# Seven-product down groups of a four-layer trunk: where the weight sums and the negated token factors stand in VectorE's order, when their loads are queued, and where ScalarE copies a first product in blocks five to eight

## The chip, the cores and the metric

One core of a Trainium2 chip runs the whole program. The time is device microseconds from one execution of the program; a run's number is a median over executions, and the kernel before was run three times. The engines that appear below are TensorE (PE; its weight loads are PEld), VectorE (DVE), ScalarE (ACT), GpSimd (POOL) and SyncE (SP). Each takes its own instructions in order. SP issues the plain loads; POOL issues the loads that add what they bring to what lies in the buffer.

## The reference

A trunk of four layers on 512 tokens of width 1024, in fp32. Each layer is a mixer (S5, gated linear attention, differential attention, S5) and then a SwiGLU feed-forward part; only the latter is touched here:

```python
def swiglu_ffn(h, w_gate_up, w_down):
    g, u = jnp.split(h @ w_gate_up, 2, axis=-1)
    return (jax.nn.silu(g) * u) @ w_down
...
        h = rmsnorm(x, norm_ffn[layer])
        x = x + swiglu_ffn(h, ffn_w_gate_up[layer], ffn_w_down[layer]).astype(x.dtype)
```

The hidden width is 2816, w_gate_up is 1024 x 5632, w_down 2816 x 1024.

## The kernel before

**Precision.** A product of fp32 matrices is made of three matmuls on rounded values: each operand is split into a high part (a rounding copy on ScalarE, L420 for weights) and a low part (the rest, a subtraction on VectorE, L428), and high x high, high x low and low x high are summed in PSUM. So each tile of weights of 128 x 1024 needs one ScalarE copy and one VectorE subtraction (`split`) before TensorE can use it.

**Blocks.** `ffn` handles the 2816 hidden columns in 11 blocks of 256. The gate and up columns of a block are computed together by `seven_block`: the two halves of the tokens and the two halves of the depth make a 2 x 2 block product, which is done with seven products and not eight (`seven_product`, L594), by sums of weights and of activations. The products are named by the method's steps: `one` writes bank a, `two` bank d, `five` bank c, and so on; the functions ending in `_out` take a bank away. In `one_out` ScalarE copies bank a to r1 (L816), `two_out` adds bank d to r1 on VectorE (L823), and `scale1` multiplies r1 by the token factors (L786).

**Down groups.** The blocks are gathered in groups of 4, 4 and 3, and each group is multiplied with its rows of w_down and added to x. In layers 2 and 3 the first two groups (blocks 0 to 3 and 4 to 7) use seven products here too (`seven_down`, L1113 for the matmuls); there `raw(b)` is the room of the block's results. Its weights are named by the same method: `1` is a sum of two quarters, made by a plain load and an accumulating load by POOL; `S` first takes a quarter and then, on VectorE, the tile `1` is added to it (L1131, "the weight sums", two tiles of 128 x 1024 per group). `11`, `21`, `22`, `3` are the others. `parts` splits the activations (L1102 on ScalarE, L1104 on VectorE). `add` adds a bank to x with the token factors r, or with their negative nr (L1154); in layer 2 r is first turned through memory (the tile rturned, brought back by a transfer), in layer 3 it stands in memory already.

**What sets the order.** The program is written in the order of the steps; a scheduler then places each instruction on its engine by what it depends on, and `issue_after` ties an instruction behind another. In the third and later blocks of `ffn` the steps come in the order of the loops that the printed code shows; `early`, `sums`, `before` and `products` are the four pieces of a down group. Loads go to SP in the order of the program's steps. A load can start when its buffer is free. The buffers are `wst` (a ring of three staged tiles), `whl` (a ring of five split tiles), and a list `slots` of eight tiles that are taken and handed back (slot0, slot1, slot2, gain, and four that are pieces of the tile halves). Matmul results go to PSUM: four banks of one kind (a, c, a2, c2), two of another (d, d2).

Of the kernel before, what the change touches and what calls it, by code (L numbers as in the profile page):

```python
# [12 lines left out]
F32 = mybir.dt.float32  # L13
# [9 lines left out]
P = 128  # L23
# [317 lines left out]
class Trunk:  # L341
# [387 lines left out]
    def seven_block(self, fp, slots, left, wgu, b, turn, na, glued, raw=None):  # L729
# [83 lines left out]

        def one_out():
            keep["r1"] = third("r1")
            nc.scalar.copy(keep["r1"][:], bank["a"][:])  # L816

        def two():
            bank["d"] = self.sbank("d")
            product("12", "21", bank["d"], True)  # L820

        def two_out():
            v.tensor_tensor(keep["r1"][:], keep["r1"][:], bank["d"][:], op=ALU.add)  # L823

        def scale1():
            scale(keep["r1"], keep["r1"], 0)
# [75 lines left out]
    def ffn(self, l, left, after=None, turn=False, aside=None, small=None):  # L902
# [7 lines left out]
        with self.tc.tile_pool(name=f"ffn{l}", bufs=1, reuse_waits="tile") as fp:  # L910
# [88 lines left out]
            for nb in (4, 4, 3) if na == 4 else (3, 3, 3, 2):  # L999
                acts = []  # L1000
                down = self.seven_down(fp, slots, rooms, wd, b0, r, na, turn) if b0 < halved else None
                for n in range(b0, b0 + nb):
                    b = blocks[n]
                    if down and n == max(b0 + 2, 3):
                        down["early"]()
# [11 lines left out]
                    if n > 2 or l == 1 and n == 2:  # L1017
                        loads(b)
                        for step in ("one", "one_out", "five", "five_out"):
                            b[step]()  # L1020
                        b["add"]("22")
                    if n > 1:
                        for step in ("six", "six_out", "two", "two_out", "scale1", "silu1", "seven", "seven_out", "three", "three_out"):
                            b[step]()
                        b["add"]("21")
                        if down and n == b0 + 3:
                            down["sums"]()
                        b["four"]()
                        if down and n == b0 + 3:
                            down["before"]()  # L1030
                        for step in ("gate2", "times"):
                            b[step]()
# [27 lines left out]
    def seven_down(self, fp, slots, rooms, wd, b0, r, na, turn):  # L1060
# [66 lines left out]
        def early():  # L1127
            load("1", 0, 1, (0, 0), True)
            load("S", 1, 1, None, True)
            for w, y in zip(W["1"], W["S"]):  # L1130
                v.tensor_tensor(y, w, y, op=ALU.add)  # L1131
# [6 lines left out]
        def sums():  # L1138
            load("11", 0, 0)
            load("21", 1, 0, None, True)  # L1140
# [7 lines left out]
        def products():  # L1148
# [4 lines left out]
            nr = self.sp.tile([P, NT], F32, tag="ms4", name="nr", bufs=2)  # L1153
            v.tensor_scalar_mul(nr[:], r[:], -1.0)  # L1154
# [6 lines left out]
            freed("21")  # L1161
# [3 lines left out]
            add(0, 0, a, r)  # L1165
            d = [self.sbank("d2") for _ in range(2)]
# [30 lines left out]
        return {"early": early, "before": before, "sums": sums, "products": products}  # L1197
# [1924 lines left out]
```

## Time and profile before

| what | value |
|---|---|
| median of 3 runs | 2228.75 us (2226.74 to 2230.62) |
| profiled execution, its own time | 2231.23 us |
| its span | 2229.5 us |
| mean granted TensorE clock | 0.992 of full speed |
| bytes moved by transfers | 354.67 MB, mean 159 GB/s |
| first down group, layer 2, from the end of blocks 0 and 1 | 1400 to 1515 us |
| second down group, layer 2 | 1515 to 1634.7 us |
| first down group, layer 3 (its end) | 1912 to 2008.8 us |
| second down group, layer 3 | 2008.8 to 2131.6 us |

A row of the timeline has the start, the length, engine, line, operation, written and read tile; brackets hold the idle time ahead of it and what ended it. A row of the waits has a total, the times and the longest. The windows give per stretch the length, the busy time of TensorE, its weight loads, VectorE, ScalarE and GpSimd with their counts, the granted clock, the busy share of the transfer engines, and GB/s. A row of the transfers has the number, the size and the median us from issue to landing.

### The profile page before, as it was taken

How to read it: one execution, taken by the hardware profiler on the slowest of the kernel's cores; microseconds unless marked ns; L12 is line 12 of the kernel's file. 1: busy time of each engine (PE TensorE's matmuls, PEld its weight loads, DVE VectorE, ACT ScalarE, POOL GpSimd, SP SyncE). 2: the span in 40 equal slices, each digit the busy share in tenths (PEclk: the TensorE clock that was granted, in tenths of full speed). 3: DMA queues.
4: the chain of work that ended last, by engine and by line, in shares of the span. 5: the costliest groups of instructions: out<-in, count | busy, mean ns of one | idle time of the engine just before them, and what ended most of it. 6: DMA issues, size and time to landing. Idle time of an engine off the chain costs nothing.

```text
span 2229.5 us, 38518 instructions
## 1 busy us (share of the span) xinstructions
PE 2156.1 (97%) x15313; PEld 1958.4 (88%) x15313; DVE 1707.8 (77%) x2588; ACT 1173.6 (53%) x1852; POOL 360.9 (16%) x467
## 2 busy tenths in 40 slices
PE   6999999999999999999999999899999999999998
PEld 5888989989988898999888888799998888889997
DVE  9965978777987597877645786797986965897885
ACT  8644635445666465564435785454553334554553
POOL 3401152340210110100002221111110001111100
PEclk9999999999999999999999999899999999999999
DMA  4357667665863686764347556979762646788752
GB/s 92 64 173 179 175 160 189 171 172 161 189 142 124 151 205 165 172 186 117 96 135 163 119 130 170 233 205 215 199 168 58 161 142 159 190 224 186 203 146 76
DMA packets 320101, 354.67 MB, mean 159 GB/s; under 512 B 71220, under 2 KB 253648, under 8 KB 319794
## 3 DMA queue, kind: packets, MB, share of 16 engines
q1 hardware_dynamic: 243362, 247.39, 36.7%
q0 software_dynamic: 76560, 104.82, 25.3%
q8 instruction: 121, 1.98, 0.4%
q14 instruction: 58, 0.48, 0.1%
HBM read 318.20 MB, written 18.75 MB: 151 GB/s over the span
## 4 chain that ended last, share of the span: by engine, by line
PE 77%; DVE 10%; DMA 5%; ACT 4%; issue 3%; SPq 1%; POOL 0%; DVEq 0%; POOLq 0%; ACTq 0%
PE a L594 20%; PE c L594 9%; PE acc L448 8%; PE acc L450 8%; PE acc L449 8%; PE d L594 5%; DVE whl L428 3%; PE a L1113 2%; PE y L1860 2%; PE acc L1896 2%; PE c L1113 1%; ACT whl L420 1%; DMA gain<-in_ffn_w_down_dram 1%; PE s L2868 1%; DMA halves<-in_ffn_w_down_dram 1%
## 5 line engine op out<-in xcount | busy, mean ns | idle before, releaser
L428 DVE TENSOR_TENSOR whl<-wst,whl 128x1024 fp32r<-128x1024 f32 x244 | 296.8, 1222 | 181.3 <-ACT whl L420 178.3
L594 PE MATMUL a<-side,whl 128*128 128x256 f32 x3240 | 401.6, 281 | 22.0 <-DVE whl L428 15.3
L594 PEld LDWEIGHTS a<-side,whl 128*128 128x128 f32 x3240 | 387.8, 192 | 25.1 <-DVE whl L428 17.1
L420 ACT CAST whl<-wst 128x1024 fp32r<-128x1024 f32 x244 | 255.5, 1051 | 203.1 <-PE acc L450 115.4
L594 PE MATMUL c<-side,whl 128*128 128x256 f32 x2160 | 263.2, 279 | 7.1 <-DVE g L786 5.5
L594 PEld LDWEIGHTS c<-side,whl 128*128 128x128 f32 x2160 | 255.2, 189 | 7.6 <-issue 5.6
L428 DVE TENSOR_TENSOR whl<-slot,whl 128x1024 fp32r<-128x1024 f32 x121 | 146.9, 1221 | 39.7 <-ACT whl L420 39.6
L448 PE MATMUL acc<-whl,act 128*128 128x512 f32 x448 | 176.1, 394 | 0.4 <-ACT whl L420 0.4
L449 PE MATMUL acc<-whl,act 128*128 128x512 f32 x448 | 174.9, 390 | 0.0
L450 PE MATMUL acc<-whl,act 128*128 128x512 f32 x448 | 174.8, 390 | 0.0
L420 ACT CAST whl<-slot 128x1024 fp32r<-128x1024 f32 x121 | 126.7, 1052 | 86.2 <-DVE slot L840 28.4
L420 ACT CAST whl<-halves 128x1024 fp32r<-128x1024 f32 x103 | 107.5, 1051 | 90.4 <-DVE halves L840 38.8
L428 DVE TENSOR_TENSOR whl<-halves,whl 128x1024 fp32r<-128x1024 f32 x103 | 125.0, 1221 | 25.2 <-ACT whl L420 24.5
L594 PE MATMUL a<-sides,whl 128*128 128x256 f32 x1080 | 132.8, 279 | 0.6 <-DVE x L576 0.6
L594 PE MATMUL d<-sides,whl 128*128 128x256 f32 x1080 | 132.0, 278 | 0.4 <-ACT whl L420 0.4
L594 PEld LDWEIGHTS a<-sides,whl 128*128 128x128 f32 x1080 | 128.6, 189 | 1.7 <-issue 1.0
L594 PEld LDWEIGHTS d<-sides,whl 128*128 128x128 f32 x1080 | 128.1, 188 | 0.6 <-ACT whl L420 0.6
L448 PEld LDWEIGHTS acc<-whl,act 128*128 128x128 f32 x448 | 84.0, 188 | 19.0 <-ACT whl L420 0.6
L450 PEld LDWEIGHTS acc<-whl,act 128*128 128x128 f32 x448 | 84.1, 188 | 17.7
L775 POOL DMA_DIRECT2D wst<-in_ffn_w_gate_up_dram x44 | 56.9, 1293 | 258.1 <-DMA wst<-in_ffn_w_gate_up_dram 94.0
L449 PEld LDWEIGHTS acc<-whl,act 128*128 128x128 f32 x448 | 84.2, 188 | 16.5
L1113 PE MATMUL a<-whl,part 128*128 128x512 f32 x384 | 89.7, 389 | 0.0
(565 smaller groups left out, 4399.2 us busy)
## 6 DMA issues: line engine op xcount, KB each, us to landing
wst<-in_ffn_w_gate_up_dram SPq DMA_DIRECT2D x88, 512.0 KB, 5.3
slot<-in_ffn_w_gate_up_dram SPq DMA_DIRECT2D x75, 512.0 KB, 5.4
wst<-in_ffn_w_down_dram SPq DMA_DIRECT2D x72, 512.0 KB, 4.6
wst<-in_ffn_w_gate_up_dram POOLq DMA_DIRECT2D x44, 512.0 KB, 6.9
halves<-in_ffn_w_gate_up_dram SPq DMA_DIRECT2D x36, 512.0 KB, 5.8
wst<-in_s_w_glu_dram SPq DMA_DIRECT2D x32, 512.0 KB, 4.8
wst<-in_diff_w_qkv_dram SPq DMA_DIRECT2D x24, 512.0 KB, 3.8
slot<-in_ffn_w_gate_up_dram POOLq DMA_DIRECT2D x16, 512.0 KB, 8.1
```

What stands on the lines that cost most here:

```text
L420: self.last["high"] = self.nc.scalar.copy(hl[:, 0], w[:])
L428: self.last["low"] = self.nc.vector.tensor_tensor(hl[:, 1], w[:], hl[:, 0].bitcast(F32), op=ALU.subtract)
L448: mm(out, lh, rh, start=first, stop=False)
L449: mm(out, lh, rl, start=False, stop=False)
L450: self.last["mm"] = mm(out, ll, rh, start=False, stop=last)
L594: mm(o, *two, start=first and not (j or k or n), stop=k == 3 and n == 2, skip_group_check=True,)
L775: nc.gpsimd.dma_start(w[:], left.quarter(*plus, b), accum_op=ALU.add)
L1113: self.last["mm"] = nc.tensor.matmul(banks[t][:], o[:, y, k, ts], hl[:, z, k % 2], start=first and not (k or n), stop=k == 3 and n == 2, s ...
L1860: mm(yb[:, b], q[:, j, b], om[:, j // 2, bs(b)], start=False, stop=j == 3)
L1896: mm(accs[t][:], zT[:, m // 2, kk, t * P : (t + 1) * P], hl[:, m % 2, kk % 2], start=kk == 0 and m == 0, stop=kk == KT - 1 and m == 2,)
L2868: nc.tensor.matmul(ss[m][:], qs[:, m, ts], ks[:, m, z], start=z == 0, stop=z == 1)
```

## The change

- `early` (the part 11 and the differences s3) is called at the third block of each group; for the first group this is one block earlier. The loads of `1` and `S` leave it; a new function `weights` holds them and is called at the group's last block, after that block's gate-up loads.
- The sums S = 1 + S leave `early` too and are made in `sums`, which is now called after `four` and not before it, and are tied behind the last weight subtraction issued by then (`last["low"]`).
- The weights `21` come through the staging ring and no longer through slots, so `freed("21")` is gone.
- nr is made after the parts 2 and tied behind their last subtraction.
- In blocks 4 to 7 (counted from 0) of layers 2 and 3 ScalarE copies bank a into bank d, the product of `two` is accumulated on it, `two_out` has no instruction, and `scale1` reads bank d.

```diff
--- before.py
+++ after.py
@@ -811,19 +811,29 @@
             bank["a"] = self.acc("a")
             product("11", "11", bank["a"], True)
 
+        upon = raw is not None and b > 3
+
         def one_out():
-            keep["r1"] = third("r1")
-            nc.scalar.copy(keep["r1"][:], bank["a"][:])
+            if upon:
+                bank["d"] = self.sbank("d")
+                nc.scalar.copy(bank["d"][:], bank["a"][:])
+            else:
+                keep["r1"] = third("r1")
+                nc.scalar.copy(keep["r1"][:], bank["a"][:])
 
         def two():
-            bank["d"] = self.sbank("d")
-            product("12", "21", bank["d"], True)
+            if not upon:
+                bank["d"] = self.sbank("d")
+            product("12", "21", bank["d"], not upon)
 
         def two_out():
-            v.tensor_tensor(keep["r1"][:], keep["r1"][:], bank["d"][:], op=ALU.add)
+            if upon:
+                keep["r1"] = third("r1")
+            else:
+                v.tensor_tensor(keep["r1"][:], keep["r1"][:], bank["d"][:], op=ALU.add)
 
         def scale1():
-            scale(keep["r1"], keep["r1"], 0)
+            scale(keep["r1"], bank["d"] if upon else keep["r1"], 0)
 
         def silu1():
             silu(keep["r1"])
@@ -1001,7 +1011,7 @@
                 down = self.seven_down(fp, slots, rooms, wd, b0, r, na, turn) if b0 < halved else None
                 for n in range(b0, b0 + nb):
                     b = blocks[n]
-                    if down and n == max(b0 + 2, 3):
+                    if down and n == b0 + 2:
                         down["early"]()
                     if not glued and n < 2:
                         if l == 2 and n == 0:
@@ -1016,6 +1026,8 @@
                             b[step]()
                     if n > 2 or l == 1 and n == 2:
                         loads(b)
+                        if down and n == b0 + 3:
+                            down["weights"]()
                         for step in ("one", "one_out", "five", "five_out"):
                             b[step]()
                         b["add"]("22")
@@ -1023,9 +1035,9 @@
                         for step in ("six", "six_out", "two", "two_out", "scale1", "silu1", "seven", "seven_out", "three", "three_out"):
                             b[step]()
                         b["add"]("21")
+                        b["four"]()
                         if down and n == b0 + 3:
                             down["sums"]()
-                        b["four"]()
                         if down and n == b0 + 3:
                             down["before"]()
                         for step in ("gate2", "times"):
@@ -1124,11 +1136,11 @@
         whole = slice(0, 4)
         us = []
 
-        def early():
+        def weights():
             load("1", 0, 1, (0, 0), True)
             load("S", 1, 1, None, True)
-            for w, y in zip(W["1"], W["S"]):
-                v.tensor_tensor(y, w, y, op=ALU.add)
+
+        def early():
             parts("11", [(whole, part(0, 0))])
             for k in (0, 2):
                 u = self.np_.tile([P, 2, 256], F32, tag="h", name="s3")
@@ -1137,7 +1149,10 @@
 
         def sums():
             load("11", 0, 0)
-            load("21", 1, 0, None, True)
+            load("21", 1, 0)
+            with self.tc.issue_after(self.last["low"].ins):
+                for w, y in zip(W["1"], W["S"]):
+                    v.tensor_tensor(y, w, y, op=ALU.add)
 
         def before():
             split("11")
@@ -1150,19 +1165,19 @@
             if turn:
                 parts("12", [(whole, part(0, 1))])
                 self.behind = {"silu": self.last["part high"], "scaled": self.last["part low"]}
-            nr = self.sp.tile([P, NT], F32, tag="ms4", name="nr", bufs=2)
-            v.tensor_scalar_mul(nr[:], r[:], -1.0)
             s1, s2, s4 = part(1, 0), part(0, 0), part(0, 1)
             for ks, y in us:
                 v.scalar_tensor_tensor(s2[:, ks], y, -1.0, part(1, 1)[:, ks], op0=ALU.mult, op1=ALU.subtract)
             self.behind = None
             a = [self.acc("a2") for _ in range(2)]
             product("11", "11", a, True)
-            freed("21")
             load("3", 0, 1, (1, 1), True)
             parts("2", [(whole, s2)])
             split("S")
             add(0, 0, a, r)
+            nr = self.sp.tile([P, NT], F32, tag="ms4", name="nr", bufs=2)
+            with self.tc.issue_after(self.last["part low"].ins):
+                v.tensor_scalar_mul(nr[:], r[:], -1.0)
             d = [self.sbank("d2") for _ in range(2)]
             product("12", "21", d, True)
             more("S", 1, 0)
@@ -1194,7 +1209,7 @@
             product("22", "S", a, False)
             add(1, 0, a, r)
 
-        return {"early": early, "before": before, "sums": sums, "products": products}
+        return {"early": early, "before": before, "sums": sums, "weights": weights, "products": products}
 
     def turn_x(self, r):
 
```

Line numbers of the changed kernel lie up to 15 higher: L1154 becomes L1180, the sums L1131 become L1155, L1104 L1116, L1122 L1134, L1135 L1147, L840 L850, L823 L833, L861 L871, L868 L878, L1077 L1089. The pieces of order below show the place of the first down group of layer 2; the other three groups move in the same way. A row gives the line, the operation, the tile written and the tiles read (with their buffer numbers), the shape, and in brackets the semaphores waited for: DMAHW and DMASW stand for transfers, PE, Activation and DVE for engines.

VectorE at the end of blocks 0 and 1, around nr, before:

```order
L428 TENSOR_TENSOR whl_14686<-gain_13567,whl_14686 128x1024 [waits Activation_49]
L241 TENSOR_TENSOR side22_14327<-halves_14151,side22_14327 128x1024 [waits Activation_49]
L840 TENSOR_TENSOR lent_14332<-lent_14332,slot0_14329 128x1024
L840 TENSOR_TENSOR lent_14332<-lent_14332,slot1_14330 128x1024
L1154 TENSOR_SCALAR nr_15300<-rturned_14551 128x4 [waits DMASW7_49]
L428 TENSOR_TENSOR whl_14716<-lent_14332,whl_14716 128x1024 [waits Activation_49]
L428 TENSOR_TENSOR whl_14720<-lent_14332,whl_14720 128x1024 [waits Activation_49]
```

and changed:

```order
L428 TENSOR_TENSOR whl_14686<-gain_13567,whl_14686 128x1024 [waits Activation_49]
L241 TENSOR_TENSOR side22_14327<-halves_14151,side22_14327 128x1024 [waits Activation_49]
L850 TENSOR_TENSOR lent_14332<-lent_14332,slot0_14329 128x1024
L850 TENSOR_TENSOR lent_14332<-lent_14332,slot1_14330 128x1024
L428 TENSOR_TENSOR whl_14716<-lent_14332,whl_14716 128x1024 [waits Activation_49]
L428 TENSOR_TENSOR whl_14720<-lent_14332,whl_14720 128x1024 [waits Activation_49]
```

The row of nr, which waits for the transfer of rturned, is gone from between the additions for the last gate-up weights of blocks 0 and 1 (the two pieces of lent) and their subtractions.

VectorE some 15 rows later, as block 2 begins, around the weight sums, before:

```order
L748 TENSOR_TENSOR raw_14801<-g2_14823,r5_14518 128x64x4 [waits Activation_49]
L748 TENSOR_TENSOR raw_14801<-g2_14823,r5_14518 128x64x4
L840 TENSOR_TENSOR halves_14151<-halves_14151 128x1024 [waits DMAHW5_49]
L1131 TENSOR_TENSOR halves_14151<-halves_14151 128x1024 [waits DMAHW1_49,DMASW1_49]
L1131 TENSOR_TENSOR slot0_14329<-gain_13567,slot0_14329 128x1024 [waits DMAHW2_49,DMASW2_49]
L428 TENSOR_TENSOR whl_14886<-halves_14151,whl_14886 128x1024 [waits Activation_49]
L786 TENSOR_TENSOR g2_14889<-a_14386,R_14598 128x512 [waits PE_49]
L428 TENSOR_TENSOR whl_14921<-slot2_14331,whl_14921 128x1024 [waits DMAHW6_49,Activation_49]
```

and changed, the same place and then block 3 with the subtractions of 11 (wst_15272 and wst_15274) and 21 (wst_15276 and wst_15278):

```order
L748 TENSOR_TENSOR raw_14801<-g2_14823,r5_14518 128x64x4
L850 TENSOR_TENSOR halves_14151<-halves_14151 128x1024 [waits DMAHW5_49]
L1147 TENSOR_TENSOR s3_14897<-raw_14801 128x512 [waits DVE_49]
L428 TENSOR_TENSOR whl_14886<-halves_14151,whl_14886 128x1024 [waits Activation_49]
L850 TENSOR_TENSOR halves_14151<-halves_14151,slot2_14331 128x1024 [waits DMAHW6_49,DVE_49]
L786 TENSOR_TENSOR g2_14889<-a_14386,R_14598 128x512 [waits PE_49]
L428 TENSOR_TENSOR whl_14928<-slot2_14331,whl_14928 128x1024 [waits Activation_49]
```

```order
L1155 TENSOR_TENSOR halves_14151<-slot0_14329,halves_14151 128x1024 [waits DMAHW7_49,DMASW2_49]
L833 TENSOR_TENSOR r1_15093<-r1_15093,d_15155 128x512 [waits PE_49]
L1155 TENSOR_TENSOR slot2_14331<-slot1_14330,slot2_14331 128x1024 [waits DMAHW5_49,DMASW3_49]
L786 TENSOR_TENSOR r1_15093<-r1_15093,R_14598 128x512 [waits DVE_49]
L428 TENSOR_TENSOR whl_15282<-wst_15272,whl_15282 128x1024 [waits DMAHW6_49,Activation_49]
L871 TENSOR_TENSOR r5_15123<-r5_15123,a_15065 128x512 [waits PE_49]
L428 TENSOR_TENSOR whl_15285<-wst_15274,whl_15285 128x1024 [waits DMAHW1_49,Activation_49]
L428 TENSOR_TENSOR whl_15288<-wst_15276,whl_15288 128x1024 [waits DMAHW3_49,Activation_49]
L878 TENSOR_TENSOR r2_15153<-c_15095,r2_15153 128x512 [waits PE_49]
L748 TENSOR_TENSOR raw_15014<-r2_15153,r1_15093 128x64x4 [waits DVE_49]
L748 TENSOR_TENSOR raw_15014<-r2_15153,r1_15093 128x64x4
L428 TENSOR_TENSOR whl_15291<-wst_15278,whl_15291 128x1024 [waits DMAHW6_49,Activation_49]
```

The two sums stood ahead of splits of block 2's weights and each waited for a plain and an accumulating transfer; in their place stand one difference s3 and, a split later, an addition of block 2's weights, and the sums stand at the end of block 3, ahead of the subtractions of 11 and 21.

SP's queue at block 3's loads, before:

```order
L1077 DMA halves_14151<-in_ffn_w_down_dram 128x2x512 [waits DMAHW7_49,DVE_49]
L1077 DMA gain_13567<-in_ffn_w_down_dram 128x2x512 [waits DMAHW0_49,DVE_49]
L1077 DMA halves_14151<-in_ffn_w_down_dram 128x2x512 [waits DMAHW1_49,DVE_49]
L1077 DMA slot0_14329<-in_ffn_w_down_dram 128x2x512 [waits DMAHW2_49,DVE_49]
L772 DMA slot1_14330<-in_ffn_w_gate_up_dram 128x4x256 [waits DMAHW3_49,DVE_49]
L409 DMA wst_15064<-in_ffn_w_gate_up_dram 128x4x256 [waits DMAHW4_49,DVE_49,Activation_49]
L409 DMA wst_15247<-in_ffn_w_down_dram 128x2x512 [waits DMAHW5_49,DMASW0_49,DVE_49]
L772 DMA halves_14151<-in_ffn_w_gate_up_dram 128x4x256 [waits DMAHW6_49,DVE_49,Activation_49]
```

and changed:

```order
L772 DMA halves_14151<-in_ffn_w_gate_up_dram 128x4x256 [waits DMAHW7_49,DVE_49]
L772 DMA gain_13567<-in_ffn_w_gate_up_dram 128x4x256 [waits DMAHW0_49,DVE_49]
L772 DMA halves_14151<-in_ffn_w_gate_up_dram 128x4x256 [waits DMAHW1_49,DVE_49]
L1089 DMA slot0_14329<-in_ffn_w_down_dram 128x2x512 [waits DMAHW2_49,DVE_49]
L1089 DMA slot1_14330<-in_ffn_w_down_dram 128x2x512 [waits DMAHW3_49,DVE_49]
L409 DMA wst_15056<-in_ffn_w_gate_up_dram 128x4x256 [waits DMAHW4_49,DVE_49,Activation_49]
L1089 DMA slot2_14331<-in_ffn_w_down_dram 128x2x512 [waits DMAHW6_49,DMAHW5_49,DVE_49]
L409 DMA wst_15272<-in_ffn_w_down_dram 128x2x512 [waits DMASW0_49,DVE_49]
L1089 DMA halves_14151<-in_ffn_w_down_dram 128x2x512 [waits DMAHW7_49,DVE_49,Activation_49]
```

The four down loads (two for 1, two for S) stood ahead of the gate-up loads of block 3; now three of block 3's loads come first, the two of 1 follow, and those of S stand behind a staged gate-up tile, with the first staged tile of 11 between them.

## The prediction

> **What bounds the kernel now.** I read the page's busy shares and the chain first, then VectorE's waits over the stretch in which the changed code works (the first two down groups of layers 2 and 3), then the timelines of both engines at those waits, and last the windows. Shares and chain say that TensorE sets the end nearly everywhere; what remains is where it stands still or runs at a lower clock.
>
> ```profile
> PE 2156.1 (97%) x15313; PEld 1958.4 (88%) x15313; DVE 1707.8 (77%) x2588; ACT 1173.6 (53%) x1852; POOL 360.9 (16%) x467
> PE 77%; DVE 10%; DMA 5%; ACT 4%; issue 3%; SPq 1%; POOL 0%; DVEq 0%; POOLq 0%; ACTq 0%
> ```
>
> Of VectorE's waits between 1400 and 2135 us, three are waits for a transfer that the down code needs, and one is its ordinary wait for ScalarE's rounding. The numbers are the sum, the times, and the longest, in us.
>
> ```profile
> DVE whl L428 <- ACT whl L420: 70.2, 53, 5.1
> DVE halves L1131 <- DMA halves<-in_ffn_w_down_dram: 19.1, 4, 7.9
> DVE nr L1154 <- DMA rturned<-rturn: 8.7, 1, 8.7
> DVE slot L1131 <- DMA gain<-in_ffn_w_down_dram: 1.9, 1, 1.9
> ```
>
> These six waits (19.1 + 8.7 + 1.9 = 29.7 us; five at the sums, one at nr) stand at four places, one in each down group. VectorE takes its instructions in order, so what waits behind a sum or behind nr is the splitting of the weights that TensorE wants next. VectorE's timeline:
>
> ```profile
> 1424.90 0.17 DVE L1154 TENSOR_SCALAR nr<-rturned 128x4 f32<-128x4 f32 x1 [8.65 <-DMA rturned<-rturn]
> ...
> 1440.07 1.23 DVE L1131 TENSOR_TENSOR slot<-gain,slot 128x1024 f32<-128x1024 f32 x1 [1.85 <-DMA gain<-in_ffn_w_down_dram]
> ...
> 1526.09 1.23 DVE L1131 TENSOR_TENSOR halves<-slot,halves 128x1024 f32<-128x1024 f32 x1 [7.91 <-DMA halves<-in_ffn_w_down_dram]
> ...
> 1927.92 1.23 DVE L1131 TENSOR_TENSOR halves<-halves 128x1024 f32<-128x1024 f32 x1 [5.75 <-DMA halves<-in_ffn_w_down_dram]
> ...
> 2021.88 1.23 DVE L1131 TENSOR_TENSOR halves<-slot,halves 128x1024 f32<-128x1024 f32 x1 [4.47 <-DMA halves<-in_ffn_w_down_dram]
> 2024.06 1.23 DVE L1131 TENSOR_TENSOR halves<-halves 128x1024 f32<-128x1024 f32 x1 [0.95 <-DMA halves<-in_ffn_w_down_dram]
> ```
>
> And TensorE's, where its idle time in brackets follows each of them by 1 to 3 us:
>
> ```profile
> 1426.25 8.39 PE L594 MATMUL a<-side,whl 128*128 128x256 f32 x46 [8.15 <-DVE whl L428]
> ...
> 1442.48 4.37 PE L594 MATMUL a<-side,whl 128*128 128x256 f32 x22 [1.94 <-DVE whl L428]
> ...
> 1528.50 2.79 PE L594 MATMUL a<-side,whl 128*128 128x256 f32 x22 [1.90 <-DVE whl L428]
> ...
> 1931.62 5.46 PE L594 MATMUL c<-side,whl 128*128 128x256 f32 x24 [5.46 <-DVE g L786]
> ...
> 2030.54 5.49 PE L594 MATMUL a<-side,whl 128*128 128x256 f32 x24 [4.93 <-DVE r L861]
> ```
>
> A stall costs twice: after four of the five gaps the granted clock is low for a while. In the windows below the third column from the right is that clock, then DMA share and GB/s.
>
> ```profile
> 1426.25:1434.60 8.35, 8.35 (x48) 8.35 (x49) 8.35 (x13) 1.86 (x3) 2.39 (x2) 0.63 1.13 289
> 1442.48:1446.85 4.37, 4.37 (x24) 4.37 (x25) 4.37 (x6) 0.74 (x2) 0.92 (x1) 0.61 1.16 178
> 1528.50:1531.00 2.50, 2.50 (x21) 2.50 (x22) 2.50 (x3) 0.00 (x0) 0.00 (x0) 1.00 0.51 149
> 1931.62:1936.90 5.28, 5.28 (x25) 5.28 (x26) 5.28 (x6) 3.61 (x5) 2.59 (x2) 0.50 0.49 77
> 2030.54:2035.80 5.26, 5.26 (x24) 5.26 (x25) 4.70 (x5) 1.46 (x2) 1.28 (x1) 0.50 0.99 152
> ```
>
> At a clock c a stretch T loses T(1 - c): 3.1, 1.7, 0, 2.6 and 2.6 us. The four groups as windows (length, then busy TensorE, weight loads, VectorE, ScalarE, GpSimd):
>
> ```profile
> 1400.00:1515.00 115.00, 104.30 (x703) 96.96 (x704) 101.30 (x121) 59.44 (x68) 19.39 (x17) 0.94 0.89 221
> 1515.00:1634.70 119.70, 116.27 (x843) 108.56 (x842) 102.81 (x117) 60.30 (x70) 17.60 (x14) 1.00 0.84 208
> 1912.00:2008.80 96.80, 91.34 (x604) 84.61 (x604) 86.86 (x96) 50.39 (x57) 14.85 (x12) 0.96 0.89 224
> 2008.80:2131.60 122.80, 117.87 (x842) 111.12 (x841) 100.77 (x109) 61.28 (x70) 17.86 (x15) 0.97 0.83 202
> ```
>
> TensorE's idle time is 10.7, 3.4, 5.5 and 4.9 us. With the clock losses each group loses 15.5 (4.8 of it clock), 3.4, 8.1 and 7.5 us: 34.5 us in all, the most that the change can give from TensorE's side.
>
> **The change part by part.**
>
> *nr leaves its place.* The multiplication (L1154) was scheduled to the end of blocks 0 and 1, ahead of two splits of their weights, and its input comes back from a transfer. It now stands behind the rounding rests of part 2, some 70 rows later; what reads the same input before it, the first accumulation of the down group, stands where it stood. This removes the 8.65 us wait of the first group of layer 2 and nothing elsewhere, since the other three nr had no wait.
>
> *The weight sums (L1131) leave the early blocks.* They were scheduled at block 2's start in first groups and within some 10 us of the start of second ones (1526.09 and 2021.88 above). Now they stand in the last block of a group, ahead of the splits of 11 and 21, and the loads are queued behind that block's gate-up loads in place of ahead of them. This removes the other five waits' places (21.0 us of VectorE). The sums themselves stay: 2 per group at 1.22 us, so VectorE's work is the same and only its place differs.
>
> How much of the 34.5 us comes back depends on VectorE, which in two groups has little to spare:
>
> ```profile
> 1416.25:1483.05 66.80, 56.65 (x427) 54.79 (x425) 54.98 (x70) 33.03 (x40) 9.22 (x8) 0.90 0.84 213
> ...
> 1943.00:1993.00 50.00, 50.00 (x340) 46.17 (x339) 48.95 (x55) 30.25 (x35) 6.12 (x5) 1.00 0.77 195
> ```
>
> In the first, 66.80 - 54.98 = 11.8 us of idle VectorE, of which 8.65 + 1.85 = 10.5 are the two transfer waits; at its end TensorE waits for VectorE's rounding of a part. So without the waits this group gains at most 10.5, not 15.5, and TensorE keeps some small gaps; I take 9. In layer 3's first group both engines are full after the stall (50.00 and 48.95 of 50), so the gain lies between VectorE's own wait of 5.75 and TensorE's 8.1: 7. In the second groups VectorE is idle for 16.9 and 22.0 us, so nearly all comes back: 3 of 3.4 and 7 of 7.5. Sum 9 + 3 + 7 + 7 = 26 us.
>
> [...]
>
> *The waits for transfers that could come in their place.* The sums' loads now have less time: the first half's buffer is released some 26 VectorE rows, over 20 us, before its sum, the second half's between 7 and 13 us before (counted in rows of the new order). The nearest landings, in the stretch 1400 to 1520 us (median us from issue):
>
> ```profile
> wst<-in_ffn_w_gate_up_dram SPq DMA_DIRECT2D x7, 512.0 KB, 10.5
> ...
> halves<-in_ffn_w_down_dram SPq DMA_DIRECT2D x6, 512.0 KB, 7.4
> ...
> wst<-in_ffn_w_down_dram SPq DMA_DIRECT2D x4, 512.0 KB, 7.5
> gain<-in_ffn_w_down_dram SPq DMA_DIRECT2D x1, 512.0 KB, 17.9
> ```
>
> 7.4 against 7 to 13 is no wait; 10.5 would be a wait of up to 3.5 in a group. I take 0.
>
> *A new chain, through the staging ring.* The weights of product 21 used to sit in slots and were loaded early; now they go through the ring of three staged tiles. The second half of 21 takes the buffer that the first half of 11 leaves, so its load starts only when VectorE has subtracted that half. In the new order five kinds of work stand between that subtraction and the one of 21's second half: an accumulation (0.68), two splits (1.22 each), another accumulation (0.67) and a product written as two pieces (1.06 together), 4.85 us. The load and ScalarE's rounding must fit in:
>
> ```profile
> L420 ACT CAST whl<-wst 128x1024 fp32r<-128x1024 f32 x244 | 255.5, 1051 | 203.1 <-PE acc L450 115.4
> ...
> wst<-in_ffn_w_down_dram SPq DMA_DIRECT2D x72, 512.0 KB, 4.6
> ```
>
> 4.6 + 1.05 - 4.85 = 0.8 us of wait by the program's median, 7.5 + 1.05 - 4.85 = 3.7 by the median of this stretch. What stands behind it on VectorE is the second gate half and a part for the first down products; on ScalarE, which waits for the load first, the rounding of the following weights. VectorE is ahead of TensorE there by a microsecond or two, so part is hidden: I take 1 us per group, 4 in all, with 0 and 14.8 as ends. If the cover is gone the higher one holds.
>
> *Blocks 5 to 8, layers 2 and 3.* ScalarE's copy goes to the bank in which the product 12x21 is then accumulated, and VectorE's addition is gone, 8 times:
>
> ```profile
> L823 DVE TENSOR_TENSOR r<-r,d 128x512 f32<-128x512 f32 x44 | 30.0, 683 | 1.2 <-PE d L594 1.2
> L786 DVE TENSOR_TENSOR r<-r,R 128x512 f32<-128x512 f32 x44 | 30.1, 688 | 0.8
> L786 DVE TENSOR_TENSOR g<-a,R 128x512 f32<-128x512 f32 x44 | 30.0, 683 | 0.3 <-PE a L594 0.3
> L816 ACT COPY r<-a 128x512 f32<-128x512 f32 x44 | 25.7, 584 | 23.7 <-PE a L594 23.7
> ```
>
> That is 8 x 0.683 = 5.5 us less of VectorE, all in the second groups, where it has 16.9 and 22.0 us to spare: 0 on the path. The scaling now reads the bank: 683 ns from a bank against 688 from memory, so no change. A copy into a bank stands in no row; by the copy out of one it takes 584 ns, and two products of TensorE lie between it and its reader. Without that cover it would be 8 x 0.58 = 4.7 us lost, with VectorE's saving fully on the path 5.5 gained; I take 0, as the cover of two products is far longer than a copy.
>
> *Sum.* 26 - 4 = 22 us off. The profiled execution took 2231.23 us (span 2229.5), so it would be 2209; it lies 2.5 above the median of the runs, 2228.75, so the changed kernel's median comes out at 2206.5.
>
> **The rivals.**
>
> *A. All of TensorE's loss comes back* (34.5 us, 2194). For it: the six waits explain all four places. Against it: VectorE at 48.95 of 50 us and the 10.5 us bound of the first group. Chance 0.12.
>
> *B. The transfers become the bound.* The same bytes must then pass in less time. The window of the first group moves 221 x 115 = 25.4 MB; in 106 us that is 240 GB/s, and layer 3's first 21.7 MB in 89.8 us 241. In the product stretch the engines were full at 243:
>
> ```profile
> 1483.05:1515.12 32.07, 32.02 (x142) 26.54 (x143) 30.44 (x33) 16.37 (x18) 7.63 (x7) 1.00 0.98 243
> ```
>
> Against it: 289 GB/s in the first clock window. If some 230 holds over a group, the first groups take 110.5 and 94.3 us, a gain of 4.5 and 2.5, and the ring's wait goes to the middle of its ends, 7 in all: 4.5 + 3 + 2.5 + 7 - 7 = 10 us, 2219. [...] Chance 0.17.
>
> *C. Slower, by the staging ring.* One mechanism, in each last block: the load of 21's second half lands late. The wait is L + 1.05 - 4.85 for a landing L, and past about 4.9 us of wait the clock loss of 2.6 comes on top (rows above). With L = 8.7 the four groups pay 4 x (4.9 + 2.6) = 30 and the gain of 26 is gone; that is the point from which it decides. With 10.5, the median of the staged gate-up loads in this stretch, 4 x (6.7 + 2.6) = 37 us, 11 more than now: 2240. Against it: 7.5 and 4.6 for the down weights themselves. Chance 0.09.
>
> *D. No change: the same waits at new places.* The sums' second halves and the ring take back about as much as is freed, 26 us, by waits near 5 us in each group with the clock held: 2229. For it, the slack of 7 us at its low end. Chance 0.07. That the edit leaves nr or the sums where they were is excluded by the new order.
>
> **How the numbers follow.** The forecast has 0.55, A 0.12, B 0.17, D 0.07, C 0.09. The forecast's own range is 2199 to 2214, from the terms: 9 to 10.5, 3 to 3.4, 5.75 to 8.1 and 6 to 7.5, less 0 to 10. The 8-in-10 range takes in A's near part and B: 2194 to 2221; what it leaves out is C, D and the end of A. A difference under 0.2% (4.5 us) cannot be told from none. Faster is the forecast with A and B, 0.84; no change 0.07; slower 0.09.
>
> **What would show it.** Right: no wait of VectorE at nr or at the sums, the five gaps of TensorE gone and the clock 1.00 at their places; the second groups last about 116 us each. The ring shows as VectorE's wait for ScalarE's rounding in the last block of a group, near 1 us; B shows as a DMA share near 1 over whole groups with many small waits; C as TensorE gaps over 5 us shortly before the down products. The prediction is wrong if the first group's gaps turn up again as many small ones, or if the sums wait for a transfer in the last block.

## The result, and the profile after

The changed kernel takes 2214.26 us (median of 4 runs, 2213.66 to 2218.14), the kernel before 2229.04 us (2226.74 to 2230.62). The ratio is 0.9938, 95% interval 0.9921 to 0.9955: 14.8 us faster, where 22 were forecast. The profiled execution has a span of 2212.3 us against 2229.5, so 17.2 us are to be found in the two traces.

The page of the changed kernel, its busy times and the chain by engine:

```profile
PE 2150.6 (97%) x15313; PEld 1949.0 (88%) x15313; DVE 1702.6 (77%) x2580; ACT 1171.6 (53%) x1852; POOL 360.0 (16%) x467
...
PE 77%; DVE 11%; ACT 4%; DMA 3%; issue 3%; POOL 1%; SPq 0%; DVEq 0%; POOLq 0%; ACTq 0%
```

VectorE has lost the eight additions (5.2 us less), and transfers have a smaller part in the chain, 3% for 5%. Waits of VectorE at nr or at the sums (L1155 now) no longer occur. What took their place is seen when each down group is cut at its first down product. The first stretch of a layer starts with TensorE's first product behind its L148 matmuls, which stand at the same place of the program in both kernels. The windows of the kernel before, alternately the blocks of a group and its down products, in layer 2 and then in layer 3:

```profile
1404.01:1476.47 72.46, 62.37 (x508) 61.97 (x506) 60.73 (x74) 36.19 (x44) 8.57 (x8) 0.91 0.86 216
1476.47:1514.96 38.49, 38.38 (x170) 31.45 (x169) 36.69 (x41) 20.91 (x22) 8.16 (x7) 1.00 1.00 248
1514.96:1596.07 81.11, 77.78 (x673) 76.99 (x672) 66.18 (x77) 39.32 (x48) 9.13 (x8) 1.00 0.76 190
1596.07:1634.57 38.50, 38.39 (x171) 31.47 (x169) 36.54 (x41) 20.99 (x22) 8.47 (x7) 1.00 1.02 247
1903.91:1970.67 66.76, 61.30 (x508) 61.13 (x506) 58.12 (x64) 35.84 (x44) 8.38 (x7) 0.95 0.75 197
1970.67:2008.76 38.09, 38.09 (x170) 31.53 (x169) 36.60 (x41) 21.10 (x22) 7.75 (x7) 1.00 1.06 257
2008.76:2093.46 84.70, 79.77 (x674) 79.57 (x672) 64.79 (x70) 41.13 (x49) 9.99 (x8) 0.96 0.76 187
2093.46:2131.55 38.09, 38.09 (x170) 31.54 (x169) 35.97 (x40) 20.14 (x21) 7.82 (x7) 1.00 1.00 236
```

The same eight stretches of the changed kernel:

```profile
1401.87:1463.61 61.74, 59.37 (x508) 58.01 (x506) 59.19 (x70) 34.77 (x43) 10.49 (x9) 1.00 1.05 263
1463.61:1508.36 44.75, 40.80 (x170) 32.94 (x169) 38.33 (x44) 21.91 (x23) 6.27 (x5) 0.92 0.86 213
1508.36:1585.67 77.31, 76.92 (x673) 76.72 (x672) 63.22 (x72) 38.39 (x47) 11.19 (x9) 1.00 0.81 197
1585.67:1627.70 42.03, 40.23 (x170) 32.52 (x169) 37.53 (x43) 21.90 (x23) 6.24 (x5) 0.96 0.89 214
1897.97:1955.91 57.94, 57.94 (x508) 57.66 (x506) 55.34 (x62) 34.72 (x43) 9.96 (x8) 1.00 0.87 230
1955.91:1999.61 43.70, 40.05 (x171) 31.15 (x169) 38.20 (x43) 20.45 (x22) 6.22 (x5) 1.00 0.89 216
1999.61:2076.26 76.65, 76.65 (x673) 76.65 (x672) 62.60 (x67) 41.56 (x51) 11.16 (x9) 1.00 0.90 216
2076.26:2114.36 38.10, 38.10 (x171) 31.55 (x170) 36.87 (x41) 20.59 (x22) 6.27 (x5) 1.00 0.87 213
```

| stretch, us | before | changed | difference |
|---|---|---|---|
| blocks, groups 1 and 2 of layer 2 | 72.46, 81.11 | 61.74, 77.31 | -10.7, -3.8 |
| blocks, groups 1 and 2 of layer 3 | 66.76, 84.70 | 57.94, 76.65 | -8.8, -8.1 |
| down products, groups 1 and 2 of layer 2 | 38.49, 38.50 | 44.75, 42.03 | +6.3, +3.5 |
| down products, groups 1 and 2 of layer 3 | 38.09, 38.09 | 43.70, 38.10 | +5.6, 0.0 |

The blocks give 31.4 us, the clock at the old gaps is 1.00, and the down products take 15.4 of it back. (The remaining 1.2 us of the spans lie outside these stretches, where the program is the same.) So the second group of layer 2 gains next to nothing in the end, 119.3 us for 119.6. The place of the loss is seen best in the first group of layer 2. The chain goes from SyncE's load of the second half of 21 to ScalarE's rounding of it, VectorE's subtraction, ScalarE's rounding of a part, and TensorE's second down product. The rows stand below by engine: SyncE, ScalarE, VectorE (first the subtraction that frees the buffer), TensorE.

```profile
1460.14 0.37 SPq L409 DMA_DIRECT2D wst<-in_ffn_w_down_dram  x1
```

```profile
1467.04 1.05 ACT L420 CAST whl<-wst 128x1024 fp32r<-128x1024 f32 x1 [6.45 <-DMA wst<-in_ffn_w_down_dram]
...
1472.08 1.99 ACT L1114 CAST part<-raw 128x1024 fp32r<-128x1024 f32 x2 [0.53 <-DVE raw L748]
```

```profile
1458.90 1.22 DVE L428 TENSOR_TENSOR whl<-wst,whl 128x1024 fp32r<-128x1024 f32 x1
...
1468.12 1.23 DVE L428 TENSOR_TENSOR whl<-wst,whl 128x1024 fp32r<-128x1024 f32 x1 [3.42 <-ACT whl L420]
```

```profile
1473.18 8.15 PE L1125 MATMUL d<-whl,part 128*128 128x512 f32 x24 [3.95 <-ACT part L1114]
```

VectorE's subtraction at 1458.90 ends at 1460.12 and frees a buffer of the ring; the load is issued at 1460.14 and has landed by 1467.04, 6.9 us later, with ScalarE idle for it; VectorE idles 3.42 us, the second half of the gate and with it the next part come late, and TensorE stands still for 3.95 us. Behind that gap the clock is low again (window 1473.18 to 1480.00, and the same place of the second group):

```profile
1473.18:1480.00 6.82, 6.82 (x19) 5.15 (x20) 6.82 (x9) 2.90 (x3) 1.20 (x1) 0.64 0.91 154
1594.28:1600.66 6.38, 6.38 (x21) 5.14 (x22) 6.38 (x8) 1.05 (x1) 0.40 (x1) 0.74 0.80 139
```

In the other groups the load landed 4.8, 8.5 and 6.0 us after its issue and VectorE waited 1.35, 4.41 and 0.95 us.

### The profile page after: what moved, and what is told of

Its sections match the earlier page's. It is cut to its first block, busy times and chain, and to the rows that moved or that the text cites. A ratio compares the mean times of both kernels' runs of the same rounds, so it can differ in the third digit from the quotient of the medians.

```text
span 2212.3 us, 38516 instructions
## 1 busy us (share of the span) xinstructions
PE 2150.6 (97%) x15313; PEld 1949.0 (88%) x15313; DVE 1702.6 (77%) x2580; ACT 1171.6 (53%) x1852; POOL 360.0 (16%) x467
## 4 chain that ended last, share of the span: by engine, by line
PE 77%; DVE 11%; ACT 4%; DMA 3%; issue 3%; POOL 1%; SPq 0%; DVEq 0%; POOLq 0%; ACTq 0%
PE a L594 19%; PE c L594 9%; PE acc L448 8%; PE acc L450 8%; PE acc L449 8%; PE d L594 5%; DVE whl L428 3%; PE a L1125 3%; PE y L1875 2%; PE acc L1911 2%; PE c L1125 2%; ACT whl L420 1%; PE s L2883 1%; DMA wst<-in_ffn_w_down_dram 1%; PE op L2916 1%
## 5 line engine op out<-in xcount | busy, mean ns | idle before, releaser
L428 DVE TENSOR_TENSOR whl<-wst,whl 128x1024 fp32r<-128x1024 f32 x252 | 306.5, 1222 | 196.8 <-ACT whl L420 195.4
L594 PE MATMUL a<-side,whl 128*128 128x256 f32 x3240 | 392.2, 277 | 5.1 <-DVE whl L428 3.3
L594 PEld LDWEIGHTS a<-side,whl 128*128 128x128 f32 x3240 | 378.7, 188 | 8.0 <-DVE whl L428 4.8
L420 ACT CAST whl<-wst 128x1024 fp32r<-128x1024 f32 x252 | 263.8, 1051 | 221.8 <-PE acc L450 117.0
```

The lines of the kernel that those rows point to most:

```text
L420: self.last["high"] = self.nc.scalar.copy(hl[:, 0], w[:])
L428: self.last["low"] = self.nc.vector.tensor_tensor(hl[:, 1], w[:], hl[:, 0].bitcast(F32), op=ALU.subtract)
L594: mm(o, *two, start=first and not (j or k or n), stop=k == 3 and n == 2, skip_group_check=True,)
```

## The experiments

Each run has the kernel before measured beside it, so runs are compared by their ratios to it; a difference between the times of two runs is rougher. There are three theories for the 15.4 us lost in the down products: the staging ring (the load can be issued only when a buffer is freed, too late); VectorE simply late, since the weight sums stand there now; the transfers, with all loads of the stretch landing late.

**The weights 21 back in slots.** The one edit of the ring's use undone:

```diff
             load("11", 0, 0)
-            load("21", 1, 0)
+            load("21", 1, 0, None, True)
...
             product("11", "11", a, True)
+            freed("21")
             load("3", 0, 1, (1, 1), True)
```

> The changed kernel with both tiles of the weights 21 back in slots (and handed back after the first down product), all else as changed. Theory 1, the staging ring: the second half of 21 no longer waits for the buffer of 11's first half, so VectorE's waits of 3.4, 1.35 and 4.4 us for its rounding go, TensorE's gaps ahead of the second down product too, and the four stretches of down products (44.75, 42.03, 43.70, 38.10 us in the changed kernel) all come to about 38.5: 13 to 15 us less than the changed kernel, 2199 to 2202 us. Theory 2, the work itself: the weight sums and one more part now stand in the last block and VectorE is simply late there; then it makes no difference where 21 lies, the gaps stay and the time is within 3 us of 2214. Theory 3, the transfers: the same bytes are bunched at the end of a group and every load lands late; then the wait moves to another load there and at most a third of the 15 us comes back.

Measured: 2202.64 us, ratio to the kernel before 0.9891 (0.9876 to 0.9906). The down products of the four groups:

```profile
1464.22:1504.94 40.72, 38.69 (x170) 31.38 (x169) 38.14 (x44) 21.75 (x23) 8.81 (x7) 1.00 1.02 248
...
1582.26:1621.11 38.85, 38.39 (x170) 31.46 (x169) 37.19 (x44) 21.11 (x22) 8.20 (x7) 1.00 0.99 238
...
1948.43:1987.60 39.17, 38.94 (x170) 31.31 (x169) 38.11 (x43) 19.81 (x21) 7.45 (x6) 1.00 1.03 247
...
2064.30:2102.40 38.10, 38.10 (x171) 31.54 (x169) 36.05 (x41) 20.14 (x21) 7.57 (x6) 1.00 1.02 236
```

They sum to 156.84 us against 168.58: 11.7 of the 15.4 us are back. The first group still lacks 2.2 us; TensorE stands still there for 1.31 and 0.72 us around the second down product. The sums stand where the change put them, so VectorE being late by its own work does not explain the loss. The transfer engines are busier over these stretches than in the changed kernel (0.99 to 1.03, there 0.86 to 0.89), so full engines alone do not explain it either. The loads of 21 no longer wait for a buffer of the ring, so the time at which these bytes move has changed too.

**Only its second tile in a slot.**

```diff
-            load("21", 1, 0)
+            load("21", 1, 0, half=True)
...
-                if keep:
+                if keep or half and j == 1:
```

(and this one tile handed back after the first down product)

> The changed kernel with only the second tile of 21 in a slot, the first through the ring. Theory 1, the staging ring: the first tile has the buffer of a gate-up tile that is split some 8 us earlier, so only the second half's wait counted; like both in slots within 3 us, 2199 to 2204 us. Theories 2 and 3: within 4 us of 2214.

Measured: 2201.11 us, ratio 0.9885 (0.9869 to 0.9900); the down products take 39.62, 38.84, 38.85 and 38.10 us, 155.41 in all. In the first group of layer 2 VectorE subtracts it at 1463.89 us without a wait, where in the changed kernel it waits 3.42 us for its rounding, and TensorE's gap of 3.95 us ahead of the second down product is 0.21:

```profile
1469.90 1.20 PE L1125 MATMUL d<-whl,part 128*128 128x512 f32 x4 [0.21 <-ACT part L1114]
```

So it is the one tile that has to wait for 11's first half. By the ratios this kernel and its combination with the next edit (below) are the fastest of the study, and with both tiles in slots (0.9891) the time cannot be told from theirs.

**The weight sums between the subtractions of 11 and 21.** This lengthens the distance between freeing the buffer and needing the load without touching the ring:

```diff
         def sums():
             load("11", 0, 0)
             load("21", 1, 0)
-            with self.tc.issue_after(self.last["low"].ins):
-                for w, y in zip(W["1"], W["S"]):
-                    v.tensor_tensor(y, w, y, op=ALU.add)
...
             split("11")
+            with self.tc.issue_after(self.last["low"].ins):
+                for w, y in zip(W["1"], W["S"]):
+                    v.tensor_tensor(y, w, y, op=ALU.add)
```

> The changed kernel with the two weight sums placed behind the subtractions of 11 and ahead of those of 21 (before: ahead of both), ring and loads as changed. Theory 1, the staging ring: the subtraction that frees the buffer comes 2.4 us earlier and the one that needs the load about as late as before, so the wait falls by about 2.4 us in each of the groups that had 3.4, 1.35 and 4.4 us, TensorE's gap shrinks as much and the clock loss behind the largest goes partly: 5 to 9 us less than the changed kernel, 2205 to 2209 us. Theory 2, VectorE late by its own work: the same instructions in the same stretch, within 2 us of 2214. Theory 3, transfers late for want of bandwidth: within 3 us of 2214.

Measured: 2214.81 us, ratio 0.9948 (0.9930 to 0.9966), no difference from the changed kernel that can be told: a miss for the 5 to 9 us that I gave to the ring's theory. Its trace tells why, in the first group of layer 2 (SyncE, ScalarE, and the window of the down products):

```profile
1458.71 0.37 SPq L409 DMA_DIRECT2D wst<-in_ffn_w_down_dram  x1
```

```profile
1468.99 1.05 ACT L420 CAST whl<-wst 128x1024 fp32r<-128x1024 f32 x1 [5.68 <-DMA wst<-in_ffn_w_down_dram]
```

```profile
1465.64:1510.54 44.90, 40.18 (x171) 32.33 (x169) 38.10 (x44) 21.91 (x23) 6.81 (x6) 0.96 0.85 216
```

The load was issued as soon as its buffer was free, but took 10.3 us to land, not 6.9, and VectorE waited 4.45 us. Counted from the first down product, the load was issued 6.9 us ahead of it here and 3.5 us ahead in the changed kernel, and landed at the same point in both, 3.4 us behind that product's start (1468.99 against 1465.64, 1467.04 against 1463.61). The earlier issue brought nothing there. The engines that move the data are full in both kernels. The window of the same 14 us, first of the changed kernel and then of this one (the last two columns are the share and GB/s):

```profile
1456.00:1470.00 14.00, 12.59 (x85) 11.10 (x83) 10.55 (x14) 3.85 (x6) 2.47 (x2) 1.00 1.08 292
```

```profile
1456.00:1470.00 14.00, 13.21 (x95) 12.06 (x94) 9.62 (x11) 4.89 (x7) 2.37 (x2) 1.00 1.06 284
```

In the two groups where the landing was 7.2 and 6.2 us the down products did get shorter, 42.03 to 40.79 and 43.70 to 40.11 us; the first group's stayed (44.75 and 44.90), and its blocks and layer 3's took 0.6 and 0.5 us longer. So the third theory seems to have its share: in the first group the load did not land sooner for being issued sooner, which fits full transfer engines, though no run here changes the traffic alone. What puts that load on the path is its late issue through the ring, as the two runs above show; with both tiles in slots the same 14 us moved 280 GB/s at a share of 0.97.

**Both at once.** The second tile in a slot, the sums between 11 and 21.

> The changed kernel with the second tile of 21 in a slot and the weight sums between the subtractions of 11 and of 21. With the ring out of the way (theory 1) the place of the sums has nothing left to free: the same as with the second tile in a slot alone, 2201 us, within 2. If VectorE's place for the sums still costs something by itself (theory 2), 1 to 3 us less.

Measured: 2203.72 us, ratio 0.9882 (0.9867 to 0.9896); the kernel before took 2229.73 beside it. By the ratios this is the same as the second tile in a slot alone: with the ring out of the way, neither of the two places of the sums can be told to cost more.

**The ring alone, in the kernel before.** The weights 21 through the ring, all else as before:

> The kernel before with the weights 21 alone sent through the staging ring (and not handed back as slots), sums and nr at their old places. In its order 7 rows, some 6.5 us, stand between the subtraction that frees the buffer and the one that needs the load. Theory 1, the ring by itself: with landings of 5 to 10 us TensorE gets a gap ahead of the second down product in two or three groups, each with a stretch of slow clock: 4 to 14 us more than the kernel before, 2233 to 2243 us. Theory 2, the ring costs only together with the loads that the change queues at the end of a group: the loads of 1 and S have long landed here, landings are 4 to 6 us, and the time is within 3 us of before.

Measured: 2230.66 us against 2227.32, ratio 1.0016 (1.0006 to 1.0026): just outside the 3 us of the second expectation and short of the 4 us of the first. In the trace its down products take 43.86, 40.32, 38.95 and 38.09 us, 8.1 more than before, with the same gap (the row of TensorE):

```profile
1482.07 7.60 PE L1113 MATMUL d<-whl,part 128*128 128x512 f32 x24 [3.61 <-ACT part L1102]
```

But its blocks take 294.5 us against 305.0, and the waits for the sums came down; two slots that 21 no longer holds are free for the next group's loads. VectorE's waits in this kernel (in the kernel before 19.1 and 8.7):

```profile
DVE halves L1131 <- DMA halves<-in_ffn_w_down_dram: 14.5, 3, 5.8
DVE nr L1154 <- DMA rturned<-rturn: 7.8, 1, 7.8
```

So the ring costs by itself, without the change's other edits. The size of what the blocks give back is not settled: the profiled execution of this run was one of its fastest (2228.44 us) and that of the kernel before was above its median (2231.23 us), so the traces differ by 2.8 us the other way than the medians. That the slots are the reason for the shorter waits, and that they help only while the sums stand early, is inferred from the order and not tested alone.

**nr alone, in the kernel before.**

```diff
-            nr = self.sp.tile([P, NT], F32, tag="ms4", name="nr", bufs=2)
-            v.tensor_scalar_mul(nr[:], r[:], -1.0)
             s1, s2, s4 = part(1, 0), part(0, 0), part(0, 1)
...
             add(0, 0, a, r)
+            nr = self.sp.tile([P, NT], F32, tag="ms4", name="nr", bufs=2)
+            with self.tc.issue_after(self.last["part low"].ins):
+                v.tensor_scalar_mul(nr[:], r[:], -1.0)
```

> The kernel before with nr alone moved behind part 2; weight sums, loads, weights 21 and banks as before. Theory 1, the waits add up: the 8.65 us wait of nr and the clock loss of 3.1 behind it go, 9 to 11 us less than before, 2217 to 2220 us. Theory 2, the stall moves on: VectorE comes some 8 us sooner to the weight sums, whose load landed at 1440 us in the kernel before and is not earlier for it, so their wait there grows from 1.85 to 7 us or more and TensorE stands still at that place instead: 0 to 4 us less than before, 2224 to 2229 us.

Measured: 2229.49 us against 2229.73, ratio 0.9999 (0.9990 to 1.0008): nothing. VectorE and TensorE of this kernel in the first group of layer 2 (of its slowest execution, 2235.87 us, the one that was profiled):

```profile
1439.07 1.23 DVE L1131 TENSOR_TENSOR halves<-halves 128x1024 f32<-128x1024 f32 x1 [8.14 <-DMA halves<-in_ffn_w_down_dram]
1442.27 1.23 DVE L1131 TENSOR_TENSOR slot<-gain,slot 128x1024 f32<-128x1024 f32 x1 [1.97 <-DMA gain<-in_ffn_w_down_dram]
```

```profile
1444.68 5.06 PE L594 MATMUL a<-side,whl 128*128 128x256 f32 x22 [10.61 <-DVE whl L428]
```

The stall of 8.65 us at nr is gone, and the next wait in VectorE's order has grown from nothing to 8.14 at the first sum: TensorE stands still once for 10.61 us, not for 8.15 and 1.94.

**nr alone back at its old place, in the changed kernel.**

> The changed kernel with nr alone at its old place. Theory 1: the 8.65 us wait and its clock loss come back in full in the first group of layer 2, 8 to 11 us more than the changed kernel, 2222 to 2225 us. Theory 2, nr is worth little by itself as the staging ring's wait behind it shrinks by as much (the loads have more time): 0 to 5 us more, 2214 to 2219 us.

Measured: 2222.95 us, ratio 0.9965 (0.9953 to 0.9978) where the changed kernel has 0.9938: 6 us by the ratios, short of the 8 to 11 expected by the first theory, though the time lies in its range of 2222 to 2225. With the sums out of the way the wait is paid in full (VectorE):

```profile
1423.14 0.17 DVE L1169 TENSOR_SCALAR nr<-rturned 128x4 f32<-128x4 f32 x1 [8.54 <-DMA rturned<-rturn]
```

and the blocks of that group take 69.22 us and not 61.74; its down products then take 44.10 and not 44.75, so little is given back there. So nr is worth 0 with the sums early and about 6 us with the sums late. No run puts the sums, or the place of their loads in the queue, back alone; what those two edits are worth without nr is open.

**Without the copy into the bank**, `upon = False`:

> The changed kernel without the copy into the bank: blocks 5 to 8 keep ScalarE's copy to memory and VectorE's addition (8 times 0.683 us). My theory: VectorE has that time to spare in the second groups, so no difference, within 2 us of 2214. Rival: VectorE is on the path there, and 3 to 5.5 us are lost.

Measured: 2214.95 us, ratio 0.9950 (0.9932 to 0.9968): no difference. The blocks of the second groups take 77.02 and 76.65 us, with the copy 77.31 and 76.65.

**The part 11 and the differences a block later in the first groups**, `n == max(b0 + 2, 3)` as before the change:

> The changed kernel with the part 11 and the differences s3 of the first groups a block later, as they were written before. Theory: the part and the differences are 2 to 3 us of VectorE that the last block of the first groups would get back, where VectorE is full, so 1 to 4 us more than the changed kernel, 2215 to 2218 us. Rival: it only moves within a stretch that the ring's wait ends anyway, within 1 us of 2214.

Measured: 2216.86 us, ratio 0.9942 (0.9927 to 0.9957): no difference that can be told. The time itself lies in the theory's range, 2215 to 2218, but the trace has nothing of its 2 to 3 us in the blocks of the first groups, which take 61.97 and 58.35 us for 61.74 and 57.94. So the rival fits better, without being settled.

## Why the prediction was right, and where it was off

*The direction and the four places* were right: the six waits are gone, the gaps and the low clock behind them too, and the time of 2214.26 us lies in the range of 2194 to 2221. It lies outside the forecast's own 2199 to 2214 by a hair, and inside what that range's terms give, as 23.75 less 10 off is 2215. The gain was 14.8 us and not 22, and two errors of opposite sign stand behind it: in the traces the blocks gave 5.4 us more than forecast and the ring took 11.4 more. That they partly cancel is luck. One sign failed: the second groups were to last about 116 us each, and took 119.3 and 114.8.

*What comes back in the blocks* was put at 9, 3, 7 and 7 us, 26 in all. It came to 10.7, 3.8, 8.8 and 8.1, 31.4. In the first group VectorE's bound of 10.5 us fits the 10.7 measured, and TensorE's 15.5 does not. In layer 3's first group I let VectorE's load hold the gain under 8.1; it did not, as its blocks now run without a gap (57.94 of 57.94 us). Most of rival A's 34.5 us did come back, to be lost again later.

*nr's 8.65 us wait* was put down as removed by nr's move. The wait does go, but the move alone is worth nothing, as the sums' loads then hold VectorE just as long; the prediction did not say this. The sum for the first group, taken with the sums moved, stood.

*The staging ring* is the step that was mis-sized: 1 us per group was taken, 4 in all, with 14.8 as the upper end, and the down products lost 15.4 us. The place, the chain and, within some 1.3 us, the formula held: landing + 1.05 - 4.85 gives 3.1, 1.0, 4.7 and 2.2 us for the landings measured, and VectorE waited 3.42, 1.35, 4.41 and 0.95. Two things were off. I went by the program's median landing of 4.6 us, while the stretch's own rows said 7.5 and 10.5; measured were 6.9, 4.8, 8.5 and 6.0, a mean of 6.6. And I took part of the wait as hidden by VectorE's lead over TensorE and added no clock; in the first group all of it reached TensorE, with 2.4 us of slow clock behind it. In layer 3's first group TensorE was idle for 3.65 us of the 5.6 lost; the rest shows as longer busy time at full clock (40.05 for 38.09 us), and which small waits make it up is not settled. With this one tile out of the ring the kernel reaches 2201.11, 25.8 us below the kernel before measured beside it, so the sum without the ring's term (26 us) is close to what the rest of the change is worth. That too is partly luck: in that run's trace the blocks give 30.6 us and the down products still take 2.2 back.

*The sums' loads* were taken to cost 0 in their late place, and no wait for a transfer shows there. *The bank* was taken at 0, and was.

*Rival B* was right about the traffic and wrong about the ceiling: the first group's blocks ran at 263 GB/s with a share of 1.05, above the 243 that I took for full. What the runs show at full engines is one late load; a bound over whole groups does not appear. *Rival C* named the mechanism that did cost, and its price came to 15.4 us, where it asked for 30 to cancel the gain and 37 for its own time. Its clock loss of 2.6 us past a wait of about 4.9 was an estimate from the kernel before, where it followed gaps of 4.93 and 5.46 us; in the changed kernel the clock was already 0.64 behind a gap of 3.95 us and 0.74 behind gaps of 1.07 and 0.73.

## What to carry to other kernels

When a wait in an in-order engine is taken away, ask which wait stands next in its order: here removing the first alone gave 0, and the change, which removes both, 10.7 us in that group's blocks. A tile that goes through a ring of three inherits the release time of the tile three places before it, and its landing must be read in the stretch where it will be issued, not as the program's median. Cut a group at a fixed event in both traces: a gain of 31 us and a loss of 15 look like a modest change in the total.

## What the runs showed of the hardware that was not expected

A gap of TensorE need not be long for the clock to fall behind it: in the second group of layer 2 of the changed kernel two gaps of 1.07 and 0.73 us were followed by 6.38 us at a clock of 0.74 (window above), about 1.7 us lost. The same place with gaps of 1.40 and 0.72 us (sums between 11 and 21) kept the full clock. First the two gaps of the changed kernel, then those of the other one and its window:

```profile
1592.36 1.20 PE L1125 MATMUL d<-whl,part 128*128 128x512 f32 x4 [1.07 <-ACT part L1114]
1594.28 6.38 PE L1125 MATMUL d<-whl,part 128*128 128x512 f32 x20 [0.73 <-DVE part L1116]
```

```profile
1594.89 1.20 PE L1125 MATMUL d<-whl,part 128*128 128x512 f32 x4 [1.40 <-ACT part L1114]
1596.81 4.81 PE L1125 MATMUL d<-whl,part 128*128 128x512 f32 x20 [0.72 <-DVE part L1116]
...
1596.81:1601.60 4.79, 4.79 (x21) 4.00 (x22) 4.79 (x7) 1.05 (x1) 0.39 (x1) 1.00 0.96 172
```

So the length of the gap alone does not tell the clock behind it. The prediction's rows and windows of the kernel before show the same: 0.61 behind a gap of 1.94 us, 1.00 behind one of 1.90 us. What decides between such cases is not shown by these runs.

The landing of a 512 KB load at the same place of the program went from 6.9 to 10.3 us between two kernels that differ by two instructions' places, at shares of 1.08 and 1.06 and 292 and 284 GB/s. The longer one is of the load that was issued 3.5 us earlier against the first down product and landed at the same point, so a landing counted from the issue is not the load's own transfer time.
